# Dividing an attention's weights in the transpose, by a diagonal matrix from ScalarE

## The chip, the cores and the metric

The kernel runs on one core of one Trainium2 chip. The metric is the device time of one execution in microseconds (us), as the median of several runs. The core has five engines that run side by side and wait for each other by semaphores: TensorE (PE in the profile, and PEld for its weight loads), VectorE (DVE), ScalarE (ACT), GpSimd (POOL) and SyncE (SP), which issues most of the transfers (DMA).

## The reference

One layer of an encoder on 1024 tokens of width 1024, in float32: a normalised and modulated input is projected to queries, keys and values of two attentions that run in parallel, their outputs are projected, gated, merged and added to x, and a gated feed-forward network follows. The dilated attention has three groups of four heads, and its outputs are combined by their log-sums; the neighbourhood attention has eight heads on a grid of 16 rows of 64 columns, with a bias for each head. What the change touches is the softmax of the latter:

```python
scores = jnp.einsum('brqhd,brkhd->bhrqk', qg, kn).astype(f32) * (dh ** -0.5) + bias[None]
scores = jnp.where(mask, scores, NEG_INF)
p = jax.nn.softmax(scores, axis=-1).astype(v.dtype)
o = jnp.einsum('bhrqk,brkhd->brqhd', p, vn)
```

## The kernel before, in words

Large products are made in three passes: each operand is split into a rounded high part on ScalarE (`whi`, L118) and the remainder on VectorE or GpSimd (`wlo`, L119), and high x high, high x low and low x high are added up in PSUM. The products that touch the softmax weights P (L495, L510) take plain float32 operands.

The attentions are cut into ten units of two heads. Units 0 to 5 are the dilated groups (kinds 0, 1 and 2, two units each), units 6 to 9 the neighbourhood attention (kind 3, "the fourth kind"). A loop over n makes the steps: step n projects one tile of 128 tokens of unit n // 8 (`proj_chunk`, L305, 24 matmuls into a bank `ps_d`), and beside it runs the attention of items of earlier units. From step 80 on, gate products (L705) stand in the place of the projection, for twelve steps.

An item of the fourth kind is 128 queries of two heads against two key blocks (first and last item of a unit) or three (the six between): 22 key blocks a unit, 88 in four units, 176 for two heads. An item passes through three steps:

- In its first step, `at_scores` multiplies q and k on TensorE (L469, into `ps_s`). Then `at_qk`, once for each head: VectorE adds the bias and finds the maximum (L483), ScalarE takes exp and the sum (L484), VectorE takes the reciprocal of the sum (L486, into column 2 of `sx`) and divides P by it (L487).
- In its second step, `at_turn` transposes P block by block on TensorE against the identity `ident` (L495, into a bank `ps_t`), and PT is copied out of the bank by ScalarE for the first head (L501) and by VectorE for the second (L499).
- In its third step, `at_pv` multiplies PT with v (L510, into `ps_v`), ScalarE copies the result (L513) and issues its transfer (L514).

P is a tile of 512 columns in four buffers; the fourth kind uses at most 384 of them. Each name of a PSUM bank has two buffers. `ps_t` is shared: behind the turns of a step, the dilated groups' results are combined through it (`combine_step`: L665 on TensorE; L673, L675 and L676 on VectorE), and so are sums of the modulation (L271 on TensorE), whose running sum VectorE makes (L294) from rows `wa` that arrive by DMA. The same step turns the q and k of the tile projected before (L370, into `ps_v`), and splits them (L392 and L393 on ScalarE, L394 and L395 on VectorE). `proj_post` normalises the tile just projected (L323, L324 and L343 on ScalarE; L326, L328 and L130 to L134 mostly on VectorE).

On TensorE the order is as written in the code: half of the projection, scores, PV, turns of q and k, turns of P, the other half with L271 and L665 in or behind it. On the other engines a scheduler sets the order in this part of the program, from its own estimate of times; each engine then runs its list strictly in that order.

A product against a diagonal matrix is also made at the start of the kernel: four of eight tiles of x are scaled so (L232, with the diagonal `xd`), the other four are turned with the identity (L234).

Of the kernel before, what the change touches and what calls it, by code (L numbers as in the profile page):

```python
# [12 lines left out]
AF = mybir.ActivationFunctionType  # L13
ALU = mybir.AluOpType
# [29 lines left out]
def hybrid_layer(ctx: ExitStack, tc: tile.TileContext, x, colp, wada1, wada2, bada2, wqkv, wg, wpa, wpb,  # L44
                 wo, w1, w2, hgain, ropeg, rope, rbias, bmask, g2r, out):
    nc = tc.nc
# [28 lines left out]
    def bank(tag):  # L75
        return ps.tile([128, 512], F32, tag=tag, name="ps_" + tag)
# [9 lines left out]
    ident = const.tile([128, 128], F32, name="ident")  # L86
# [5 lines left out]
    for i in (0, 2):  # L92
        nc.vector.scalar_tensor_tensor(hg[:, i:i + 1], hg[:, i:i + 1], 0.125, hg[:, i + 1:i + 2],
                                       op0=ALU.mult, op1=ALU.mult)
# [213 lines left out]
    def urgent(off):  # L308
        def deco(f):
            def g(*a):  # L310
                with tc.high_priority(off):
                    return f(*a)
            return g
        return deco
# [157 lines left out]
    @urgent(AQ)  # L472
    def at_qk(I, h):
        U, nq = I.U, I.nq
        nk = I.nkb * 128
        pS = I.pS[h]
        P = I.P[h] = ap_.tile([128, 512], F32, tag="p", bufs=4, name="P")
        if U.kind < 3:
            nm, sm = U.st[:nq, I.item, h:h + 1], U.st[:nq, I.item, 2 + h:3 + h]
        else:  # L480
            sx = ap_.tile([128, 3], F32, tag="sx", bufs=4, name="sx")
            nm, sm = sx[:nq, 0:1], sx[:nq, 1:2]
        nc.vector.tensor_tensor_reduce(P[:nq, :nk], pS[:nq, :nk], I.masks[h], -1.0, 3.0e38, ALU.add, ALU.min, nm)  # L483
        nc.scalar.activation(P[:nq, :nk], P[:nq, :nk], AF.Exp, scale=-1.0, bias=nm, accum_out=sm)  # L484
        if U.kind == 3:
            nc.vector.reciprocal(sx[:nq, 2:3], sm)  # L486
            nc.vector.tensor_scalar(P[:nq, :nk], P[:nq, :nk], sx[:nq, 2:3], None, op0=ALU.mult)  # L487

    @urgent(AT)
    def at_turn(I, h):  # L490
        nq, nkb = I.nq, I.nkb
        P = I.P[h]
        pt = bank("t")
        for i in range(nkb):
            nc.tensor.transpose(pt[:, i * 128:i * 128 + nq], P[:nq, i * 128:(i + 1) * 128], ident[:nq, :nq])  # L495
        PT = I.PT[h] = ap_.tile([128, 4, 128], F32, tag="pT", bufs=4, name="PT")
        src = pt.rearrange("p (b q) -> p b q", q=128)[:, :nkb, :nq]
        if h:
            nc.vector.tensor_copy(PT[:, :nkb, :nq], src)  # L499
        else:  # L500
            nc.scalar.activation(PT[:, :nkb, :nq], src, AF.Copy)  # L501
# [413 lines left out]
    for n in range(6, 92):  # L915
# [55 lines left out]
        if n >= PAIRED or n % 2 or n < 10:  # L971
            for I in cur:
                if I.__class__ is Cluster:
                    cl_scores(I)
                    cl_qk(I)
                else:
                    at_scores(I)
                    at_qk(I, 0)
                    at_qk(I, 1)
            for I in done:  # L980
                (cl_pv if I.__class__ is Cluster else at_pv)(I)
            for j in range(0, len(turns), 2):
                qk_turns(turns[j:j + 2], "s" if n < 10 else "v")
            for I in prev:
                if I.__class__ is Cluster:
                    cl_turn(I)
                else:
                    at_turn(I, 0)
                    at_turn(I, 1)
# [263 lines left out]
    for t in range(8):  # L1253
        pbs = [bank("dsv"[t % 3]) for _ in range(2)]
        ko = KFIRST if t == 0 else (KLAST if t == 7 else range(KT))
        for n, k in enumerate(ko):
            for hf in range(2):
                for a, b in PASS:
                    nc.tensor.matmul(pbs[hf], h2T[a][:, k, t * 128:(t + 1) * 128], wow[hf, k][b],  # L1259
                                     start=(n == 0 and (a, b) == PASS[0]), stop=(n == KT - 1 and (a, b) == PASS[2]))  # L1260
# [398 lines left out]
```

## Time and profile before

| | |
|---|---|
| median of 3 runs | 1508.05 us (1505.69 to 1510.28) |
| the profiled execution | 1513.64 us |
| its span, first to last instruction | 1511.8 us |
| mean granted TensorE clock | 0.997 |
| attention of the fourth kind, first to last turn of P (L495) | 375.6 to 610.2 us |
| instructions of L487, VectorE's division of P | 64 |

The profile is of one execution. Times are from the span's start. A view of groups gives for each: line, engine, operation, output<-input, shapes and count, then busy time in us and the mean of one in ns, then the engine's idle time just before them and what ended it. A view of the timeline gives start and length in us, engine, line and count, with idle time in brackets. The duration of a matmul in the trace runs from its issue to its end, and the next one is issued long before that, so the distance from start to start is its pace.

### The profile page before, as it was taken

The page shows a single profiled execution, that of the slowest core. Times are in us where ns is not written, and L with a number is a line of the kernel's source. Part 1 is how long each engine was busy: PE and PEld are TensorE (multiplying, and loading weights), DVE is VectorE, ACT ScalarE, POOL GpSimd, SP SyncE. Part 2 cuts the span into 40 slices and gives each one's busy share as a digit, 9 for nine tenths or more (in the row PEclk, how much of TensorE's full clock was granted, in tenths as well). Part 3 has the DMA queues.
Part 4 walks back from the last instruction along what each step waited for, and adds up shares of the span by engine and source line. Part 5 has one row for each costly group of instructions (what it writes and reads, how often), then busy time and mean ns, then how long its engine had stood idle before and what let it go on. Part 6 is the DMA issues. An engine that isn't in the chain of part 4 may idle for free.

```text
span 1511.8 us, 24199 instructions
## 1 busy us (share of the span) xinstructions
PE 1486.6 (98%) x8156; PEld 1266.7 (84%) x8156; DVE 1087.9 (72%) x2265; ACT 669.9 (44%) x1691; POOL 535.6 (35%) x540
## 2 busy tenths in 40 slices
PE   8999999999999999999999999999999999999998
PEld 7999989998888877788888888888888888887886
DVE  6868777767888744466665497788767777599468
ACT  5656656555645554245532344233222333344442
POOL 0432333221100040001351311677767776104464
PEclk9999999999999999999999999999999999999999
DMA  9626444645235164833553235335433334798343
GB/s 365 232 80 190 144 145 145 190 137 166 76 114 176 47 192 135 308 106 123 176 178 143 87 96 182 119 132 180 157 130 105 109 108 146 269 366 288 99 150 103
DMA packets 150637, 241.65 MB, mean 160 GB/s; under 512 B 26464, under 2 KB 69088, under 8 KB 149744
## 3 DMA queue, kind: packets, MB, share of 16 engines
q1 hardware_dynamic: 131936, 226.45, 45.7%
q10 hardware_dynamic: 18576, 13.64, 2.8%
q8 instruction: 65, 1.06, 0.3%
q14 instruction: 60, 0.49, 0.1%
HBM read 179.89 MB, written 60.15 MB: 159 GB/s over the span
## 4 chain that ended last, share of the span: by engine, by line
PE 79%; DMA 8%; DVE 7%; ACT 3%; issue 2%; POOL 1%; SPq 0%; ACTq 0%; DVEq 0%
PE ps_d L305 11%; PE ps_v L1324 7%; PE ps_d L1324 7%; PE ps_s L1324 7%; PE ps_t L1324 6%; PE ps_d L705 4%; PE ps_s L1494 3%; PE ps_d L1494 3%; DMA wa<-in_wada_dram 3%; PE ps_v L1494 2%; PE ps_t L1494 2%; PE ps_s L1259 2%; PE ps_d L1259 2%; DVE wlo L119 2%; PE ps_v L1259 1%
## 5 line engine op out<-in xcount | busy, mean ns | idle before, releaser
L119 POOL TENSOR_TENSOR wlo<-raw,whi 128x512 fp32r<-128x512 f32 (+2 forms) x133 | 172.5, 1310 | 467.4 <-ACT whi L118 428.8
L118 ACT ACTIVATE whi<-raw 128x512 fp32r<-128x512 f32 (+1 forms) x348 | 203.9, 599 | 261.4 <-PE ps_s L1494 39.4
L305 PE MATMUL ps_d<-whi,hT 128*128 128x384 f32 x1152 | 312.0, 342 | 0.6 <-ACT vs L343 0.6
L119 DVE TENSOR_TENSOR wlo<-raw,whi 128x512 fp32r<-128x512 f32 (+1 forms) x215 | 181.9, 859 | 77.1 <-ACT whi L118 72.5
L305 PEld LDWEIGHTS ps_d<-whi,hT 128*128 128x128 f32 x1152 | 210.8, 189 | 6.1 <-ACT vs L343 4.4
L305 PE MATMUL ps_d<-wlo,hT 128*128 128x384 f32 x576 | 193.8, 337 | 2.4 <-DVE wlo L119 2.1
L305 PEld LDWEIGHTS ps_d<-wlo,hT 128*128 128x128 f32 x576 | 109.2, 190 | 3.1 <-DVE wlo L119 2.4
L118 ACT ACTIVATE whi<-ws 128x512 fp32r<-128x512 f32 x65 | 40.8, 628 | 128.2 <-DVE ws L1341 85.4
L1274 POOL TENSOR_TENSOR e<-e,c 128x512 f32<-128x512 f32 x44 | 68.8, 1563 | 61.0 <-DVE c L1404 36.8
L335 POOL TENSOR_TENSOR ra<-qn,rtab 128x64 f32<-128x64 f32 x48 | 16.2, 338 | 154.5 <-DVE qn L328 137.5
L119 POOL TENSOR_TENSOR wlo<-m,whi 128x512 fp32r<-128x512 f32 x35 | 51.3, 1477 | 54.2 <-ACT whi L118 54.2
L1272 ACT ACTIVATE e<-e 128x512 f32<-128x512 f32 x44 | 27.4, 630 | 85.2 <-DVE e L1407 58.1
L548 ACT ACTIVATE P<-P,st 128x256 f32<-128x256 f32 (+2 forms) x100 | 45.8, 459 | 36.9 <-DVE st L546 36.9
L705 PE MATMUL ps_d<-hT,whi 128*128 128x512 f32 x192 | 60.5, 397 | 0.0
L129 ACT ACTIVATE ry<-ss,eps 128x4 f32<-128x4 f32 (+1 forms) x88 | 26.3, 298 | 75.0 <-DVE ss L326 62.5
L1324 PE MATMUL ps_v<-h2T,whi 128*128 128x512 f32 x192 | 59.2, 389 | 0.0
L1324 PE MATMUL ps_s<-h2T,whi 128*128 128x512 f32 x192 | 59.1, 389 | 0.0
L294 DVE SCALAR_TENSOR_TENSOR acc<-wa,cact,acc 128x512 f32<-128x512 f32 x56 | 42.0, 750 | 21.0 <-DMA wa<-in_wada_dram 20.8
L484 ACT ACTIVATE P<-P,sx 128x384 f32<-128x384 f32 (+1 forms) x64 | 37.1, 581 | 44.9 <-DVE sx L483 44.7
L1324 PE MATMUL ps_d<-h2T,whi 128*128 128x512 f32 x184 | 56.7, 390 | 0.0
L119 DVE TENSOR_TENSOR wlo<-ws,whi 128x512 fp32r<-128x512 f32 x45 | 50.6, 1125 | 8.1 <-ACT whi L118 8.1
L1273 DVE TENSOR_TENSOR e<-e 128x512 f32<-128x512 f32 x44 | 42.5, 974 | 16.6 <-ACT e L1272 16.6
(445 smaller groups left out, 3956.9 us busy)
## 6 DMA issues: line engine op xcount, KB each, us to landing
raw<-in_w_dram SPq DMA_DIRECT2D x139, 256.0 KB
ga_d<-e SPq DMA_DIRECT2D x77, 256.0 KB
raw<-ga_d SPq DMA_DIRECT2D x77, 256.0 KB
wa<-in_wada_dram SPq DMA_DIRECT2D x32, 512.0 KB
raw<-in_wqkv_dram SPq DMA_DIRECT2D x80, 192.0 KB
m<-in_w_dram SPq DMA_DIRECT2D x44, 256.0 KB
raw<-in_wg_dram SPq DMA_DIRECT2D x42, 256.0 KB
xt<-in_x_dram SPq DMA_DIRECT2D x16, 512.0 KB
```

The source lines that it names most:

```text
L118: nc.scalar.activation(hi[:, :n], r, AF.Copy)
L119: (eng or nc.gpsimd).tensor_sub(lo[:, :n], r, fview(hi[:, :n]))
L294: nc.vector.scalar_tensor_tensor(ada_acc[c], wa, cact[:, kk:kk + 1], ada_acc[c], op0=ALU.mult, op1=ALU.add)
L305: nc.tensor.matmul(pd[:, :384], tok(a, k, t), U.w[k][b][:, :384], start=(k == 0 and i == 0), stop=(k == KT - 1 and i == 2))
L484: nc.scalar.activation(P[:nq, :nk], P[:nq, :nk], AF.Exp, scale=-1.0, bias=nm, accum_out=sm)
L548: nc.scalar.activation(C.P[h][:nq, c], C.P[h][:nq, c], AF.Exp, scale=-1.0, bias=nm, accum_out=sm)
L705: nc.tensor.matmul(st["p"], gw[i, br][j][a][:, kk * 128:(kk + 1) * 128], hT[b][:, k, hs], start=(k == 0 and q == 0), stop=(k == 7 and q == 2))
L1259: nc.tensor.matmul(pbs[hf], h2T[a][:, k, t * 128:(t + 1) * 128], wow[hf, k][b], start=(n == 0 and (a, b) == PASS[0]), stop=(n == KT - 1 an ...
L1273: nc.vector.tensor_mul(sg, sg, a)
L1274: nc.gpsimd.tensor_mul(sg, sg, up)
L1324: nc.tensor.matmul(pb, w[p][:, k * 128:(k + 1) * 128], b[q][:, k], start=(k == 0 and i == 0), stop=(k == 3 and i == 2))
L1494: nc.tensor.matmul(pb[m], o[0][a][:, m * 128:(m + 1) * 128], o[1][b], start=(k == 0 and i == 0), stop=(k == HT - 1 and i == 2))
```

## The change

For the fourth kind, VectorE no longer divides P. ScalarE instead writes a diagonal matrix into the unused columns 384 to 511 of the P tile: the identity with each row scaled by the reciprocal sum of that query. The transpose of P becomes an ordinary product of P with this diagonal, which transposes and divides in one. The other kinds keep the transpose against the identity. The rest of the program is as before; lines below the change are four higher (L499 becomes L503, L501 becomes L505, L513 becomes L517, L673 becomes L677).

```diff
         nc.scalar.activation(P[:nq, :nk], P[:nq, :nk], AF.Exp, scale=-1.0, bias=nm, accum_out=sm)
         if U.kind == 3:
             nc.vector.reciprocal(sx[:nq, 2:3], sm)
-            nc.vector.tensor_scalar(P[:nq, :nk], P[:nq, :nk], sx[:nq, 2:3], None, op0=ALU.mult)
+            nc.scalar.activation(P[:, 384:512], ident, AF.Identity, scale=sx[:, 2:3])
...
         pt = bank("t")
         for i in range(nkb):
-            nc.tensor.transpose(pt[:, i * 128:i * 128 + nq], P[:nq, i * 128:(i + 1) * 128], ident[:nq, :nq])
+            if I.U.kind == 3:
+                nc.tensor.matmul(pt[:, i * 128:(i + 1) * 128], P[:, i * 128:(i + 1) * 128], P[:, 384:512],
+                                 start=True, stop=True)
+            else:
+                nc.tensor.transpose(pt[:, i * 128:i * 128 + nq], P[:nq, i * 128:(i + 1) * 128], ident[:nq, :nq])
```

The scheduler orders VectorE and ScalarE anew around it. On VectorE, in the first step with a combine (near 420 us in the profile), the rows before are these; `P_6178` and `P_6184` are the two heads of the item in its first step, `PT_6217` is the second head's PT of the item in its second step:

```order
L134 SCALAR_TENSOR_TENSOR ry_6138<-rz_6139,ry_6138 128x4
L486 RECIPROCAL sx_6179<-sx_6179 128x1
L328 TENSOR_TENSOR qn_6131<-qn_6131,ry_6138 128x256
L487 TENSOR_SCALAR P_6178<-P_6178,sx_6179 128x256
L486 RECIPROCAL sx_6185<-sx_6185 128x1
L499 COPY PT_6217<-ps_t_6213 128x384
L487 TENSOR_SCALAR P_6184<-P_6184,sx_6185 128x256
L394 SCALAR_TENSOR_TENSOR qk_5316<-ps_v_6200,hg_87,qk_5316 128x2x64
L395 TENSOR_TENSOR qk_5316<-ps_v_6200,qk_5316 128x2x64
L673 TENSOR_TENSOR oacc_6050<-ut_6051,ps_t_6234 128x512
```

And of the change, at the same place on VectorE:

```order
L134 SCALAR_TENSOR_TENSOR ry_6138<-rz_6139,ry_6138 128x4
L328 TENSOR_TENSOR qn_6131<-qn_6131,ry_6138 128x256
L486 RECIPROCAL sx_6179<-sx_6179 128x1
L486 RECIPROCAL sx_6185<-sx_6185 128x1
L394 SCALAR_TENSOR_TENSOR qk_5316<-ps_v_6200,hg_87,qk_5316 128x2x64
L395 TENSOR_TENSOR qk_5316<-ps_v_6200,qk_5316 128x2x64
L503 COPY PT_6217<-ps_t_6213 128x384
L677 TENSOR_TENSOR oacc_6050<-ut_6051,ps_t_6234 128x512
```

The two divisions are gone, and PT's copy has moved behind the two instructions that split q and k. On ScalarE, in the same step, the rows before are these:

```order
L484 ACTIVATE P_6178,sx_6179<-P_6178,sx_6179 128x256
L513 ACTIVATE stg_6197<-ps_v_6190 128x128
L484 ACTIVATE P_6184,sx_6185<-P_6184,sx_6185 128x256
L392 ACTIVATE qk_5316<-ps_v_6200,hg_87 128x2x64
L393 ACTIVATE qk_5316<-ps_v_6200 128x2x64
L514 DMA o_d_75<-stg_6197 128x128
L501 ACTIVATE PT_6211<-ps_t_6207 128x384
L323 ACTIVATE sq_6241<-ps_d_6157 128x256
```

And of the change, at the same place on ScalarE:

```order
L484 ACTIVATE P_6178,sx_6179<-P_6178,sx_6179 128x256
L484 ACTIVATE P_6184,sx_6185<-P_6184,sx_6185 128x256
L517 ACTIVATE stg_6197<-ps_v_6190 128x128
L392 ACTIVATE qk_5316<-ps_v_6200,hg_87 128x2x64
L393 ACTIVATE qk_5316<-ps_v_6200 128x2x64
L487 ACTIVATE P_6178<-ident_89,sx_6179 128x128
L505 ACTIVATE PT_6211<-ps_t_6207 128x384
L487 ACTIVATE P_6184<-ident_89,sx_6185 128x128
L518 DMA o_d_75<-stg_6197 128x128
L323 ACTIVATE sq_6241<-ps_d_6157 128x256
```

The two diagonals stand on either side of the first head's copy of PT, and the output's transfer is issued behind them. TensorE's list differs only in the operands of L495: the second operand is P's own last 128 columns in place of `ident`.

## The prediction

> **What bounds the kernel now.** The page comes first: its busy shares, and the chain of work that ended last.
>
> ```profile
> PE 1486.6 (98%) x8156; PEld 1266.7 (84%) x8156; DVE 1087.9 (72%) x2265; ACT 669.9 (44%) x1691; POOL 535.6 (35%) x540
> PE 79%; DMA 8%; DVE 7%; ACT 3%; issue 2%; POOL 1%; SPq 0%; ACTq 0%; DVEq 0%
> ```
>
> TensorE is busy nearly always and holds 79% of the chain; VectorE holds 7%. These are means over many stages, so the second view is the table of stretches. The change touches only the attention of the fourth kind, between 374 and 616 us. Columns: length, then busy time (with instruction count) of PE, PEld, DVE, ACT and POOL, the granted clock, DMA share, GB/s.
>
> ```profile
> 400.00:440.00 40.00, 38.16 (x273) 34.10 (x273) 34.98 (x112) 21.51 (x75) 5.67 (x5) 0.96 0.48 148
> 440.00:480.00 40.00, 39.43 (x294) 34.41 (x291) 36.23 (x120) 21.79 (x76) 3.66 (x3) 1.00 0.42 125
> 480.00:520.00 40.00, 36.22 (x255) 32.04 (x255) 32.41 (x104) 19.84 (x71) 2.59 (x2) 0.96 0.34 103
> 520.00:560.00 40.00, 40.00 (x249) 31.66 (x248) 20.61 (x68) 21.38 (x62) 13.98 (x11) 1.00 0.51 152
> 616.00:1512.00 896.00, 888.22 (x3948) 733.67 (x3946) 647.78 (x854) 330.22 (x575) 402.86 (x277) 1.00 0.48 160
> ```
>
> Up to 520 us VectorE is nearly full too (36.23 of 40); after that it is half idle, while TensorE is full. Behind 616 us TensorE is busy 888 of 896 us: what the stage loses or gains reaches the end. A busy PE can hide gaps, since each matmul's recorded duration overlaps the next. So the third view is the timeline (start, length, engine, line, count): does TensorE issue at its own pace?
>
> ```profile
> 440.38 0.44 PE L370 MATMUL ps_v<-ident,qn 128*128 128x128 f32 x2
> 440.66 0.82 PE L495 MATMUL ps_t<-ident,P 128*128 128x128 f32 x6
> 441.23 0.42 PE L305 MATMUL ps_d<-whi,hT 128*128 128x384 f32 x1
> ```
>
> The six turns of one item follow the two turns of q and k without a gap, and the projection follows them. In an ordinary step the order of TensorE's own instructions sets the time. Its true stalls in the stage are in the view of waits (who waited for whom, total us, times, longest; 372 to 617 us):
>
> ```profile
> PE ps_t L665 <- DVE PT L499: 3.7, 2, 1.9
> PE ps_t L495 <- DVE oacc L676: 1.9, 1, 1.9
> PE ps_v L370 <- DVE qn L328: 1.0, 1, 1.0
> PE ps_t L271 <- DVE PT L499: 0.4, 1, 0.4
> PE ps_t L665 <- ACT PT L501: 0.2, 1, 0.2
> ```
>
> These are 7.2 us, nearly all on VectorE. Two stretches above have a clock of 0.96: 0.04 x 40 = 1.6 us of full speed lost in each, and the timeline shows it right behind a long stall (498.75) as slow matmuls:
>
> ```profile
> 496.03 0.51 PE L305 MATMUL ps_d<-whi,hT 128*128 128x384 f32 x2
> ...
> 498.75 0.66 PE L665 MATMUL ps_t<-ident,fb 128*128 128x128 f32 x4 [1.86 <-DVE PT L499]
> ...
> 501.05 0.84 PE L305 MATMUL ps_d<-whi,hT 128*128 128x384 f32 x2
> ```
>
> A pair that took 0.51 us takes 0.84. So the stage holds 7.2 + 2 x 1.6 = **10.4 us** that a lighter VectorE could at most give back.
>
> **The change part by part: TensorE.** Per key block and head, a turn against the identity (L495) becomes a real float32 product of P with the diagonal. The trace has that product already, with the same shapes: x against a diagonal, L232 (count, then ns min/median/max, first and last start).
>
> ```profile
> L232 PE MATMUL ps_d<-xd,xt x32: 275/275/377, 9.2 to 16.5; 128*128 128x128 f32 x32
> ...
> L232 PE MATMUL ps_v<-xd,xt x16: 275/275/275, 11.1 to 12.8; 128*128 128x128 f32 x16
> ...
> L232 PE MATMUL ps_s<-xd,xt x16: 275/275/377, 12.9 to 14.7; 128*128 128x128 f32 x16
> ```
>
> ```profile
> 11.12 1.95 PE L232 MATMUL ps_v<-xd,xt 128*128 128x128 f32 x16
> ```
>
> The program has 176 turns (4 head pairs x 22 key blocks x 2 heads) and the trace 110 + 66 = 176 (the table below). Of L232 it has 32 products (four token tiles of eight), and the trace 32 + 16 + 16 = 64: a float32 product runs as two instructions. Their pace: (1.95 - 0.275) / 15 = 0.112 us, so 0.224 a product; a turn's pace is (0.82 - 0.273) / 5 = 0.110. Each block costs 0.114 us more, and **176 x 0.114 = +20.1 us**, 0.68 us in a step of six. Nothing lies over it: TensorE is the engine that is waited for. By place:
>
> ```profile
> 374.00:520.00 146.00, 15.49 (x110) 12.62 (x110) 0.98 0.35 106
> 520.00:616.00 96.00, 9.67 (x66) 7.15 (x66) 1.00 0.51 153
> ```
>
> 110 blocks (12.5 us) fall where VectorE is nearly full, 66 (7.5 us) where it isn't.
>
> The Trainium skill, "TensorE: Matmul & The Clock Gate", section Back-to-back issue gap, gives about 81 ns a matmul for a sustained stream of loads and matmuls of 128 columns. By it the term would be, as an estimate, 176 x (0.162 - 0.110) = 9.2 us; the rows here show 112 ns for float32, and the row decides.
>
> **VectorE and ScalarE.** VectorE loses 64 divisions:
>
> ```profile
> L487 DVE TENSOR_SCALAR P<-P,sx 128x384 f32<-128x384 f32 x48 | 23.4, 488 | 1.2
> ...
> L487 DVE TENSOR_SCALAR P<-P,sx 128x256 f32<-128x256 f32 x16 | 7.7, 489 | 0.1
> ```
>
> 23.4 + 7.7 = 31.1 us of busy time, which counts only through the stalls above. ScalarE gains 64 activations of 128x128. The nearest rows are these:
>
> ```profile
> L392 ACT ACTIVATE qk<-ps_v,hg 128x128 fp32r<-128x128 f32 x23 | 10.9, 475 | 0.4 <-PE ps_v L370 0.3
> ...
> L513 ACT ACTIVATE stg<-ps_v 128x128 f32<-128x128 f32 x32 | 8.4, 261 | 8.8 <-PE ps_v L510 8.7
> ```
>
> So 64 x 0.26 = 16.7 us to 64 x 0.475 = 30.4 us; it cannot be below nothing, as nothing is taken from ScalarE. I take 17, by L513, the same types in plain order. It costs the end nothing while its cover holds: ScalarE is idle 18 of 40 us, and the turn that reads the diagonal comes a step later. Where the division of an item ended (421.15 + 0.34), that item's turn began only at 427.17:
>
> ```profile
> 421.15 0.34 DVE L487 TENSOR_SCALAR P<-P,sx 128x256 f32<-128x256 f32 x1
> ```
>
> ```profile
> 427.17 0.60 PE L495 MATMUL ps_t<-ident,P 128*128 128x128 f32 x4
> ```
>
> That leaves 5.7 us for ScalarE. The diagonal now waits for the reciprocal on VectorE, and behind it in ScalarE's queue stand PT's copy (L501) and the copies of the next projection (L323, L324, L343). If VectorE is late, PT's copy is late and with it the bank that L665 wants; up to all 17 us would then be on the path. I take 0.
>
> **How much of the 10.4 us comes back.** Four places, from the timeline of VectorE, and one of ScalarE:
>
> ```profile
> 373.96 0.61 DVE L487 TENSOR_SCALAR P<-P,sx 128x256 f32<-128x256 f32 x2
> 374.48 0.41 DVE L326 TENSOR_REDUCE ss<-sq 128x4 f32<-128x256 f32 x1
> ```
>
> ```profile
> 417.33 1.54 DVE L294 SCALAR_TENSOR_TENSOR acc<-wa,cact,acc 128x512 f32<-128x512 f32 x2 [1.35 <-DMA wa<-in_wada_dram]
> ...
> 420.36 0.35 DVE L487 TENSOR_SCALAR P<-P,sx 128x256 f32<-128x256 f32 x1
> 420.62 0.15 DVE L486 RECIPROCAL sx<-sx 128x1 f32<-128x1 f32 x1
> ```
>
> ```profile
> 465.35 0.43 DVE L394 SCALAR_TENSOR_TENSOR qk<-ps_v,hg,qk 128x128 fp32r<-128x128 f32 x1
> 465.68 0.40 DVE L395 TENSOR_TENSOR qk<-ps_v,qk 128x128 fp32r<-128x128 f32 x1
> 465.97 0.30 DVE L656 COPY fb<-fe 128x256 f32<-128x256 f32 x1
> ```
>
> ```profile
> 486.05 0.75 DVE L294 SCALAR_TENSOR_TENSOR acc<-wa,cact,acc 128x512 f32<-128x512 f32 x1 [0.76 <-DMA wa<-in_wada_dram]
> ```
>
> ```profile
> 496.18 0.63 ACT L118 ACTIVATE whi<-raw 128x512 fp32r<-128x512 f32 x1 [1.64 <-DMA raw<-in_wg_dram]
> ```
>
> At 375 the two divisions stand right ahead of what TensorE waits for: 374.48 - 373.96 = 0.5 of the 1.0 us comes back. At 421 only one division goes (0.26, start to start), and PT's copy is put behind L394 and L395, 0.62 us; the root there is a DMA 1.35 us late. At 487 no division is in the way, and a DMA is 0.76 late. At 499 ScalarE sat behind a DMA for 1.64. So most of the stalls are late transfers, which a lighter VectorE doesn't mend. Longer steps may: each gives a transfer 0.68 us more. I take half of 421 and 499 with their slow clock (3.7 + 3.2 = 6.9, so 3.4), 1.0 of 1.9 at 487, 0.5 at 375 and 0.3 of the rest: **-5.2 us**, between 0 and -10.4.
>
> **Sum.** +20.1 - 5.2 = +14.9. The profiled execution took 1513.64 us (span 1511.8 and 1.8 around it); 1528.5 on that scale. It lay 5.6 above the median of the runs shown, 1508.05, so the forecast is 1508.05 + 14.9 = **1523.0 us**.
>
> **Rivals.** *No stall goes, or new ones come.* The late transfers and the new place of PT's copy speak for it. +20.1 gives 1528.2; with two more stalls like that at 499 (1.9 + 1.6 each) +27.1, 1535.
>
> *All stalls go.* VectorE is 2 x 0.488 = 0.98 us lighter a step and steps are longer. +20.1 - 10.4 = +9.7: 1517.8. Against it: the roots are transfers.
>
> *VectorE sets the length of a step up to 520 us (the other side).* Then the 12.5 us of products there fall into time that TensorE has to wait anyway, 7.5 remain, and the stalls go: 7.5 - 10.4 = -2.9, 1505.2, no change. It decides if TensorE stands idle 0.68 us in every step of that stretch. For it: 36.23 of 40 us busy. Against it: 39.43 of 40 on TensorE and no gap around L495 at 440 us. The Trainium skill, "Perfetto Trace Analysis", section Optimizing Scalar/DVE Operations, says that moving work to Scalar may make sense where DVE is saturated; by that rule this rival holds, and the trace bears out the busy share, but not the waits.
>
> *The product costs no more than a turn* (one pass, so the change does less than it says): 176 x 0.002 - 5.2 = -4.8, 1503.2, faster. L232's doubled count is against it.
>
> **How the numbers follow.** Forecast 0.55, no stall goes or new ones 0.20, all go 0.15, VectorE sets the step 0.06, one pass 0.04. A measurement of this kernel can tell about 0.3%, 4.5 us, from no change: slower is the first three, 0.90; same 0.06; faster 0.04. The range runs from 1514, with room under "all go" for a cheaper product and the 2.3 us by which the runs before lie off their median, to 1533, most of the way through "new ones"; the last two rivals (0.10) and the top of the second are left out.
>
> **What would show it.** The product's line with 352 instructions at a pace of 0.112 us, and steps 0.7 us longer with no gap around it, show the main term; 176 instructions, or a pace near 0.055, refute it. VectorE some 31 us lighter in 374 to 616, ScalarE some 17 heavier. Waits of TensorE in the stage near 3.6 instead of 7.2 us, and at most one slow-clock stretch, show the share that comes back. Waits of PT's copy on ScalarE's diagonal, or stalls behind 616 us that shrink by more than 1 us, would make it wrong.

## The result, and the profile after

| | before | after |
|---|---|---|
| median | 1507.91 us (4 runs, 1505.69 to 1510.28) | 1525.45 us (4 runs, 1524.51 to 1529.0) |
| the profiled execution | 1513.64 us | 1526.08 us |
| its span | 1511.8 us | 1524.3 us |
| first to last turn or product of P | 375.6 to 610.2 us | 373.8 to 622.1 us |

The ratio is 1.0117, with an interval of 1.0101 to 1.0133. By the medians the change is 17.5 us slower. The forecast was 14.9 us slower, 1523.0 in a range of 1514 to 1533.

The page after, busy shares and the chain that ended last:

```profile
PE 1505.2 (99%) x8332; PEld 1285.6 (84%) x8332; DVE 1065.1 (70%) x2201; ACT 686.9 (45%) x1755; POOL 536.1 (35%) x540
PE 79%; DMA 8%; DVE 6%; ACT 3%; issue 2%; POOL 1%; SPq 1%; ACTq 0%; DVEq 0%
```

TensorE has 8332 - 8156 = 176 instructions more; VectorE has lost 64, ScalarE has gained 64. The same stretches after (columns as before the change: length, then busy us and count of PE, PEld, DVE, ACT, POOL, the clock, DMA share, GB/s):

```profile
400.00:440.00 40.00, 39.23 (x293) 35.69 (x292) 32.21 (x99) 24.30 (x84) 5.39 (x5) 1.00 0.46 145
440.00:480.00 40.00, 39.97 (x297) 35.09 (x296) 30.72 (x101) 23.97 (x82) 3.30 (x3) 1.00 0.36 107
480.00:520.00 40.00, 38.60 (x287) 34.63 (x287) 31.13 (x97) 22.21 (x77) 2.58 (x2) 1.00 0.40 121
616.00:1512.00 896.00, 893.03 (x3982) 737.62 (x3981) 643.77 (x853) 332.01 (x581) 403.03 (x277) 1.00 0.49 161
```

VectorE has fallen from 36.23 to 30.72 of 40 us in the middle one, ScalarE has risen from 21.79 to 23.97, and TensorE has only become fuller. The clock of 0.96 in two stretches is gone. An ordinary step on TensorE (timeline: start, length, engine, line, count) and the product's line (ns min/median/max, first and last start):

```profile
449.44 0.44 PE L370 MATMUL ps_v<-ident,qn 128*128 128x128 f32 x2
449.71 1.50 PE L496 MATMUL ps_t<-P 128*128 128x128 f32 x12
450.97 0.42 PE L305 MATMUL ps_d<-whi,hT 128*128 128x384 f32 x1
```

```profile
L496 PE MATMUL ps_t<-P x352: 275/275/377, 373.8 to 622.1; 128*128 128x128 f32 x176
```

Where six turns took 441.23 - 440.66 = 0.57 us up to the next line's start, twelve instructions for the same six blocks take 450.97 - 449.71 = 1.26, again without a gap: 0.69 us more in a step. And the waits of TensorE in the stage (who waited for whom, total us, times, longest):

```profile
PE ps_t L669 <- DVE PT L503: 1.2, 1, 1.2
PE ps_v L370 <- DVE qn L328: 1.2, 1, 1.2
PE ps_t L669 <- ACT PT L505: 0.8, 1, 0.8
PE ps_t L496 <- DVE rv L130: 0.2, 1, 0.2
```

That is 3.4 us in place of 7.2.

### The profile page after: what moved, and what is told of

It reads as the page before. It is cut to its first block, busy times and chain, and to the rows that moved or that the text cites. A ratio compares the mean times of both kernels' runs of the same rounds, so it can differ in the third digit from the quotient of the medians.

```text
span 1524.3 us, 24580 instructions
## 1 busy us (share of the span) xinstructions
PE 1505.2 (99%) x8332; PEld 1285.6 (84%) x8332; DVE 1065.1 (70%) x2201; ACT 686.9 (45%) x1755; POOL 536.1 (35%) x540
## 4 chain that ended last, share of the span: by engine, by line
PE 79%; DMA 8%; DVE 6%; ACT 3%; issue 2%; POOL 1%; SPq 1%; ACTq 0%; DVEq 0%
PE ps_d L305 12%; PE ps_v L1328 7%; PE ps_d L1328 7%; PE ps_s L1328 7%; PE ps_t L1328 6%; PE ps_d L709 4%; PE ps_t L496 2%; PE ps_s L1498 2%; PE ps_d L1498 2%; PE ps_s L1263 2%; PE ps_d L1263 2%; PE ps_t L1498 2%; PE ps_v L1498 2%; DMA wa<-in_wada_dram 2%; DVE wlo L119 2%
```

## The experiments

Two questions were put. Is the second instruction of the product the whole cost, or have the diagonal, its wait and the new order a part? And what of the price came back, and by what: the lighter VectorE, or the longer steps? Ratios are to the kernel before, run beside each experiment on the same chip; 0.001 is 1.5 us. The median of before was not the same beside all of them (1507.9 to 1509.7 us), so runs are compared by their ratios.

| run | what differs from before | ratio | interval |
|---|---|---|---|
| the change | product, diagonal on ScalarE, no division on VectorE | 1.0117 | 1.0101 to 1.0133 |
| e1 | product against the identity, VectorE divides | 1.0117 | 1.01 to 1.0135 |
| e2 | turns, no division at all | 0.9996 | 0.9983 to 1.0009 |
| e3 | turns, ScalarE divides | 0.9958 | 0.9942 to 0.9974 |
| e4 | nothing; one more execution of before | - | - |
| e6 | the change, first two units | 1.0045 | 1.0029 to 1.0061 |
| e7 | the change, last two units | 1.0054 | 1.0039 to 1.007 |
| e8 | turns of P ahead of those of q and k | 0.9984 | 0.9972 to 0.9995 |
| e9 | the change, product in one instruction | 0.9971 | 0.9955 to 0.9987 |
| e10 | e3 and e8 | 0.9962 | 0.9947 to 0.9977 |
| e11 | e9 and e8 | 0.999 | 0.9976 to 1.0004 |
| e12 | each turn made twice | 1.0108 | 1.0091 to 1.0125 |

### e1: the product alone

```diff
-            nc.tensor.transpose(pt[:, i * 128:i * 128 + nq], P[:nq, i * 128:(i + 1) * 128], ident[:nq, :nq])
+            if I.U.kind == 3:
+                nc.tensor.matmul(pt[:, i * 128:(i + 1) * 128], P[:, i * 128:(i + 1) * 128], ident, start=True, stop=True)
+            else:
+                nc.tensor.transpose(pt[:, i * 128:i * 128 + nq], P[:nq, i * 128:(i + 1) * 128], ident[:nq, :nq])
```

> The turn of the fourth kind becomes the float32 product, but against the identity, and VectorE keeps its division. Theory A (the product's second instruction is the cost, 176 x 0.114 = 20.1 us, and a lighter VectorE gives a little back): with VectorE as heavy as before, 1508 + 20 less at most 3 for the longer steps, so 1525 to 1528, as long as the change or up to 3 us longer. Theory B (VectorE sets the length of a step up to 520 us): the products there are hidden, at most 1508 + 7.5 = 1516. Theory C (the cost of the change lies in ScalarE's diagonal and the wait for it): near 1508 here.

Measured: 1528.25 us, ratio 1.0117, the same as the change (before was at 1509.69 beside it). Its waits of TensorE in the stage:

```profile
PE ps_v L370 <- DVE qn L328: 1.5, 1, 1.5
PE ps_t L668 <- DVE PT L502: 1.5, 1, 1.5
PE ps_t L668 <- ACT PT L504: 1.0, 1, 1.0
PE ps_t L496 <- DVE oacc L679: 0.2, 1, 0.2
```

These are 4.2 us where before has 7.2 (5.8 in a second profile, e4), with VectorE as heavy as before. So the product by itself costs all that the change costs, and the stalls shrink without a lighter VectorE. Theories B and C fall: they asked for at most 1516 and for 1508.

### e2: no division, and e3: ScalarE divides

```diff
-            nc.vector.tensor_scalar(P[:nq, :nk], P[:nq, :nk], sx[:nq, 2:3], None, op0=ALU.mult)
```

> P of the fourth kind is not divided at all: the turns stay, VectorE loses its 64 divisions and nothing takes their place. Theory A: only the stalls can shrink, by about 5 of the 10.4 us that the profiled execution held, so 1501 to 1506. Theory B (VectorE sets the step): 64 x 0.3 to 0.49 us less on VectorE would show nearly in full up to 520 us, so 1490 to 1496. If the stalls are late transfers alone: 1507 to 1509.

```diff
-            nc.vector.tensor_scalar(P[:nq, :nk], P[:nq, :nk], sx[:nq, 2:3], None, op0=ALU.mult)
+            nc.scalar.activation(P[:nq, :nk], P[:nq, :nk], AF.Identity, scale=sx[:nq, 2:3])
```

> ScalarE divides P in place of VectorE, with the turns as before: 64 activations of some 0.58 us, 37 us more on ScalarE. Theory A: ScalarE is half idle and the turns come a step later, so it hides; the time is that of the kernel without division, 1502 to 1507. Theory C (work added to ScalarE in this stage costs the end): above 1512.

Measured: e2 1509.12 us, ratio 0.9996: taking 31 us of instructions off VectorE (25 us of its busy time, 1087.9 to 1062.7), and putting them nowhere, gains nothing that can be measured. Theory A's 1501 to 1506 did not come; the time lies near the range of "late transfers alone". e3 measured 1503.59, ratio 0.9958: 6 us faster, with as light a VectorE and a heavier ScalarE. The two differ in where the division is, and so in the order that the scheduler made. Most of the waits of e2 and then of e3:

```profile
PE ps_t L664 <- DVE PT L498: 3.9, 2, 2.1
PE ps_t L494 <- DVE oacc L675: 1.1, 1, 1.1
```

```profile
PE ps_t L665 <- DVE PT L499: 1.1, 1, 1.1
PE ps_t L495 <- ACT qk L393: 0.9, 1, 0.9
```

There are two long waits for PT's copy in e2 and one in e3. The first is in both: 2.1 us near 420 us in e2 and 1.1 us in e3, behind rows `wa` for which VectorE sat idle 3.17 and 2.06 us. The second, 1.8 us, is in e2 alone. VectorE's timeline there, in e2 and then in e3:

```profile
493.81 0.42 DVE L394 SCALAR_TENSOR_TENSOR qk<-ps_v,hg,qk 128x128 fp32r<-128x128 f32 x1
494.14 0.37 DVE L395 TENSOR_TENSOR qk<-ps_v,qk 128x128 fp32r<-128x128 f32 x1
494.44 0.41 DVE L498 COPY PT<-ps_t 128x256 f32<-128x256 f32 x1
```

```profile
490.51 0.41 DVE L499 COPY PT<-ps_t 128x256 f32<-128x256 f32 x1
...
492.32 0.45 DVE L394 SCALAR_TENSOR_TENSOR qk<-ps_v,hg,qk 128x128 fp32r<-128x128 f32 x1
492.66 0.40 DVE L395 TENSOR_TENSOR qk<-ps_v,qk 128x128 fp32r<-128x128 f32 x1
```

In e2 the copy stands behind the split of q and k; in e3 it stands ahead. ScalarE, which had sat idle for transfers in both (1.8 us in e2, 1.4 in e3), ended its part of the split in e3 (L393) only at 491.91, so that a copy behind the split could not have begun before 492.5. At this step an earlier place of one row goes with 1.8 us less stall, where 31 us less on VectorE had gained nothing. All waits of the stage together are 6.2 us in e2 and 3.0 in e3, and their stages from first to last turn 230.4 and 227.3 us; the rest of the 6 us is not explained by these.

### e4: the kernel before, profiled again

> The kernel before, unchanged, for a second profile. If its stalls of 7.2 us on TensorE and the two stretches at a clock of 0.96 belong to every execution, they show again and the span is near 1512. If they vary, the waits are shorter, the clock 1.00, and the span near 1506, which would mean that the change had less to give back in the median than in the profiled execution.

Measured: 1506.82 us in one execution, span 1505.0. The stage is shorter than in the first profile, the clock is 1.00 throughout it, and the waits are 5.8 us:

```profile
PE ps_t L665 <- DVE PT L499: 3.5, 2, 2.1
PE ps_v L370 <- DVE qn L328: 1.0, 1, 1.0
PE ps_t L495 <- DVE oacc L676: 0.7, 1, 0.7
PE ps_t L271 <- DVE PT L499: 0.4, 1, 0.4
PE ps_t L665 <- ACT PT L501: 0.2, 1, 0.2
```

```profile
L495 PE MATMUL ps_t<-ident,P x176: 272/273/329, 373.7 to 603.9; 128*128 128x128 f32 x176
```

From first to last turn it takes 603.9 - 373.7 = 230.2 us, where the first profile had 234.6. The change's 622.1 - 373.8 = 248.3 is 18.1 more than this: about the 17.5 of the medians. So the two stretches at a clock of 0.96 and 1.4 us of the waits do not belong to every execution. But this one isn't the typical one either: it is 2.9 us below the median of the 17 runs of before beside it. Their mean clock goes from 0.996 (the slowest, 1514.56 us) to 1.000 (the fastest, 1504.72), and in the runs of the change it is 0.999 or 1.000.

### e6 and e7: half of the units each

Each is the change under a condition: `pair < 2` in e6 and `pair >= 2` in e7, at both places of its diff.

> The change for the first two of the four units alone (88 of 176 products, in the stretch in which VectorE is nearly full). Theory A (each product costs its second instruction wherever it stands): 88 x 0.114 = 10.0 us less the 1 to 3 us that late transfers gain from longer steps, so 1514 to 1518 against 1507.9 before. Theory B (what falls into the full stretch is hidden): 1505 to 1509.

> The change for the last two units alone (88 products, mostly where VectorE is half idle and TensorE has no stalls). Theory A: +10.0 us with nearly nothing given back, 1516 to 1519. Together with the first two units' it should make the whole change's 17.5 us. Theory B: 1518 here and nothing for the first two.

Measured: 1517.28 us, ratio 1.0045 (+6.8 us at 1507.9), and 1518.72 us, ratio 1.0054 (+8.1). Against the medians of before beside them (1508.64) it is 8.6 and 10.1 us; the two ways of counting differ by 2 us. Nothing is hidden where VectorE is nearly full: theory B falls again. The first half may give back a little more than the second, as expected, but the intervals (some 2.4 us to each side) don't tell the two apart, nor their sum (14.9, or 18.7 by the medians) from the whole's 17.5.

### e9: the product in one instruction

```diff
-        P = I.P[h] = ap_.tile([128, 512], F32, tag="p", bufs=4, name="P")
+        P = I.P[h] = ap_.tile([128, 512], F32 if U.kind < 3 else F32R, tag="p", bufs=4, name="P")
```

> The change with P and the diagonal as fp32r, so that the scores, P and the diagonal are rounded; everything else as in the change. If the cost is that a float32 product runs as two instructions, the trace shows 176 in place of 352 and the time falls by at least 176 x 0.112 = 19.7 us from the change's 1525.5, to 1504 to 1507, or lower if one instruction is faster than a turn. If the cost were in the diagonal, the wait or the order, it stays above 1515.

Measured: 1504.7 us, ratio 0.9971. The diagonal, its wait and the lighter VectorE are all there, and the cost is gone: 1.0117 - 0.9971 = 0.0146, 22 us, where 176 x 0.112 = 19.7 was expected; the two intervals of 0.0016 don't tell these apart. The product's line (the view writes f32 for a product of either kind):

```profile
L496 PE MATMUL ps_t<-P x176: 272/276/328, 375.8 to 604.4; 128*128 128x128 f32 x176
```

### e8, e10 and e11: the copy ahead of the split

In each step of the fourth kind (`n >= PAIRED`) the loop over `turns` (with `qk_turns`) is moved behind the loop over `prev` (with `at_turn`):

```diff
-            for j in range(0, len(turns), 2):
+            for j in range(0, 0 if n >= PAIRED else len(turns), 2):
                 qk_turns(turns[j:j + 2], "s" if n < 10 else "v")
             for I in prev:
...
                     at_turn(I, 0)
                     at_turn(I, 1)
+            for j in range(0, len(turns) if n >= PAIRED else 0, 2):
+                qk_turns(turns[j:j + 2], "s" if n < 10 else "v")
```

> The kernel before, with the turns of P written ahead of the turns of q and k in each step of the fourth kind, so that VectorE copies PT before it splits q and k in every step; the same work. If the stalls of L665 on PT's copy come from the copy standing behind a split that waits for ScalarE, the stall of 1.9 us near 494 to 499 us goes and the time falls by 2 to 5 us, to 1503 to 1506. If the stalls are set by the late transfers alone: 1507 to 1509. Slower if q and k, now turned later, hold up the scores.

Measured: 1507.94 us, ratio 0.9984, 2.4 us faster with an interval of 0.8 to 4.2; the medians alone differ by 0.7 (before was at 1508.64 beside it), and 1507.94 itself lies in the range of "late transfers alone". At the step near 494 us the wait is 0.2 us, where the second profile of before had 2.1; this is the timeline of e8 and then of before:

```profile
494.16 0.66 PE L665 MATMUL ps_t<-ident,fb 128*128 128x128 f32 x4 [0.22 <-ACT PT L501]
```

```profile
493.98 0.66 PE L665 MATMUL ps_t<-ident,fb 128*128 128x128 f32 x4 [2.12 <-DVE PT L499]
```

The place of the copy is only a part of that difference. VectorE up to the copy, in the second profile of before and then in e8:

```profile
489.59 1.25 DVE L132 TENSOR_TENSOR rz<-ry,rv 128x4 f32<-128x4 f32 x1
...
491.72 1.17 DVE L133 SCALAR_TENSOR_TENSOR rz<-rz,ry 128x4 f32<-128x4 f32 x1
492.81 0.43 DVE L394 SCALAR_TENSOR_TENSOR qk<-ps_v,hg,qk 128x128 fp32r<-128x128 f32 x1
...
493.51 0.41 DVE L499 COPY PT<-ps_t 128x256 f32<-128x256 f32 x1
```

```profile
491.71 0.15 DVE L132 TENSOR_TENSOR rz<-ry,rv 128x4 f32<-128x4 f32 x1
...
492.73 0.53 DVE L133 SCALAR_TENSOR_TENSOR rz<-rz,ry 128x4 f32<-128x4 f32 x1
493.19 0.41 DVE L499 COPY PT<-ps_t 128x256 f32<-128x256 f32 x1
```

The split ahead of the copy took 493.51 - 492.81 = 0.70 us. Before it the rows L132 and L133 together took 1.74 us more than in e8, and each ends within 0.03 us of a subtraction of GpSimd (the last section comes back to this). So in these two executions two small rows that ran long make more of the difference than the copy's place. In the first profile of before they did not run long (0.16 and 0.31 us); there the split waited for ScalarE, and the copy with it:

```profile
497.58 0.44 DVE L394 SCALAR_TENSOR_TENSOR qk<-ps_v,hg,qk 128x128 fp32r<-128x128 f32 x1 [1.62 <-ACT qk L393]
```

In e8's list of waits stands one of 2.6 us for the copy elsewhere (near 421 us, where VectorE sat idle 3.24 us for `wa`; in the second profile of before it was 0.92):

```profile
PE ps_t L665 <- DVE PT L499: 2.6, 1, 2.6
```

> ScalarE divides P (as in the run in which it does so alone, 0.9958 of the time before) and the turns of P are written ahead of the turns of q and k (alone 0.9984). If the first gained because the copy of PT came ahead of the split at the step near 494 us, the second adds little: 1501 to 1504. If the two remove different stalls, 1499 to 1502. Above 1506 if the gain of the first came from its own order, which the new writing undoes.

> The one-instruction product (fp32r, with scores, P and diagonal rounded; alone 0.9971) with the turns of P ahead of the turns of q and k. TensorE has the same work as before, VectorE 31 us less, ScalarE 25 us more. If what is left of the stalls in the one-instruction run (1.3 us on PT's copy, 0.6 on q and k) is order: 1501 to 1504. If it is late transfers: as without, 1504 to 1506.

Measured: e10 1503.17 us, ratio 0.9962, as e3 alone, so the new writing adds nothing to it in all: e3 had put the copy ahead at that step by itself. No wait for the copy is left in e10, but its list has three others, of 1.6, 1.2 and 0.9 us. e11 1507.54, ratio 0.999, is not better than e9 (its interval reaches e9's) and above both ranges; its waits are 1.9 and 1.6 us, where e9 had 2.5 in all. Why was not followed further.

### e12: each turn twice

```diff
-            nc.tensor.transpose(pt[:, i * 128:i * 128 + nq], P[:nq, i * 128:(i + 1) * 128], ident[:nq, :nq])
+            for _ in range(2 if I.U.kind == 3 else 1):
+                nc.tensor.transpose(pt[:, i * 128:i * 128 + nq], P[:nq, i * 128:(i + 1) * 128], ident[:nq, :nq])
```

> The kernel before with each turn of the fourth kind made twice into the same place: 176 more instructions at a turn's pace of 0.110 us, 19.4 us of TensorE, no product, no diagonal, VectorE divides as before. If the change costs what its second instruction costs, and the 2 to 3 us that come back of it are what longer steps give to late transfers and late copies, this comes to 1508 + 17 = 1524 to 1526 too, with waits on VectorE near 4 us in place of 7.2. If what comes back hangs on the lighter VectorE: 1527 to 1528.

Measured: 1525.41 us, ratio 1.0108, +16.3 us of a gross 19.4, with waits of 1.5 + 1.2 + 1.0 + 0.2 = 3.9 us:

```profile
PE ps_t L666 <- DVE PT L500: 1.5, 1, 1.5
PE ps_t L666 <- ACT PT L502: 1.2, 1, 1.2
PE ps_v L370 <- DVE qn L328: 1.0, 1, 1.0
PE ps_t L496 <- DVE oacc L677: 0.2, 1, 0.2
```

176 more instructions on TensorE, as turns or as halves of a product, do what the change does, and about as much of the price comes back as there, with VectorE dividing all the while.

## Why the prediction was right, and what in it was mis-sized

- **TensorE, +20.1 us**: right. 352 instructions in place of 176, at (1.50 - 0.275) / 11 = 0.111 us each; a step is 0.69 us longer, 0.68 was forecast. e1 and e12 give the cost without the rest of the change, e9 gives the rest without the cost.
- **What comes back, -5.2 us**: the sign was right and the size was not. It was a half of the 10.4 us seen in one execution. That execution was 5.6 us above the median, as the prediction itself noted; the second profile has a clock of 1.00 throughout the stage and waits of 5.8 us. After the change there are 3.4, so 2.4 come back, and 20.1 - 2.4 = 17.7, against 17.5 measured. That is again one execution each, and so close a match is partly luck: a thousandth of the mean clock, which differs between the runs, is 1.5 us. From the profiled execution before it is 1526.08 - 1513.64 = 12.4, so that 7.7 of the 20.1 came back there; the forecast of 14.9 lies in the middle, 2.5 and 2.6 us from the two. The step that failed is the carrying over of a term, worked out from the stalls of a single execution, to the median of the runs.
- **By what it comes back**: the prediction gave longer steps most of the part and the lighter VectorE some (0.5 us at 375 us, 0.26 at 421). e2 shows no gain from the lighter VectorE alone, and at 375 us the wait is 1.2 after and 1.0 before. Longer steps suffice, as e1 and e12 show. By place, in the first profile of before, the second and after: near 421 us 1.8, 1.4 and 0.8; near 487 us 1.9, 0.7 and none; near 499 us 1.9, 2.1 and 1.2.
- **The 31 us of VectorE and the 17 of ScalarE**: VectorE's busy time fell by 22.8 us (1087.9 to 1065.1), not by 31, since the 31.1 adds up durations that overlap the next row's. ScalarE's rose by just 17.0 (669.9 to 686.9), but that is luck: a diagonal takes 395 ns, not 261, so 64 x 0.395 = 25 us, and overlap makes it less. It is hidden, as e9 shows:

```profile
L487 ACT ACTIVATE P<-ident,sx 128x128 f32<-128x128 f32 x64 | 24.6, 395 | 4.1 <-DVE sx L486 4.0
```

- **The signs that it named**: TensorE waits 0.8 us for ScalarE's copy of PT near 423 us, and a diagonal stands right ahead of that copy; but e1, with no diagonal, has 1.0 us there. Behind the stage nothing is gained: from the last turn to the end of the span 901.6 and 901.1 us in the two profiles of before, 902.2 after.
- **The rivals**: VectorE as the bound up to 520 us fell with e1, e2 and e6; the cheap product fell with the trace itself. "No stall goes", 1528.2, was 2.7 us too high, about as far off as the forecast was too low, though stalls did go. "All go" was too cheap by 7.6 us.
- **The rule of the Trainium skill** on moving work to Scalar where DVE is saturated ("Perfetto Trace Analysis", Optimizing Scalar/DVE Operations) was bound to the third rival. e3 does gain by moving the division to ScalarE, 6 us, but e2 gains nothing by leaving it out. So it is not the load on VectorE that held this stage; near 494 us the traces of e2 and e3 point to order in its place.

e3 beats both kernels: 0.9958 of the time before, at no cost on TensorE. That the place of PT's copy is a part of its gain is seen against e2 at the step near 494 us (1.8 us); the rest of the 6 us was not taken apart.

## What to carry to other kernels

Folding a scale into a transpose turns one instruction of TensorE into a real product, and in float32 that was two instructions here: where TensorE sets the pace, count its instructions first, and leave the scale on an engine with room. Removing work from an engine that is only nearly full can gain nothing (e2) where the others wait for it because of late transfers, the order of its list, or rows that are held up. And a term that is read from the stalls of one profiled execution has to be checked against a second and scaled to the median, since part of them differs from one execution to the next.

## What the runs showed of the hardware

An instruction of 128 columns has nearly the same pace on TensorE in the three forms seen here: 0.110 us for a float32 turn, 0.112 for half of a float32 product and, in e9, (0.86 - 0.276) / 5 = 0.117 for an fp32r product:

```profile
446.38 0.86 PE L496 MATMUL ps_t<-P 128*128 128x128 f32 x6
```

A short VectorE instruction can be held up by GpSimd. After the change, near 498 us, VectorE's timeline and then GpSimd's:

```profile
498.16 1.04 DVE L132 TENSOR_TENSOR rz<-ry,rv 128x4 f32<-128x4 f32 x1
...
500.34 1.33 DVE L328 TENSOR_TENSOR qn<-qn,ry 128x256 f32<-128x256 f32 x1
```

```profile
497.88 1.30 POOL L119 TENSOR_TENSOR wlo<-raw,whi 128x512 fp32r<-128x512 f32 x1 [27.03 <-ACT whi L118]
500.11 1.28 POOL L119 TENSOR_TENSOR wlo<-raw,whi 128x512 fp32r<-128x512 f32 x1 [0.93 <-ACT whi L118]
```

L132 takes 0.16 us in the median; here it ends at 499.20, with GpSimd's subtraction (499.18). L328, usually 0.4, ends at 501.67 against 501.39. In the second profile of before the two long rows shown with e8 end at 490.84 and 492.89, and GpSimd's subtractions at 490.82 and 492.87. Which row is held changes with the time at which the transfer ahead of the subtraction lands. The Trainium skill ("Perfetto Trace Analysis", Optimizing Scalar/DVE Operations) says that GPSIMD and DVE share an SBUF read port, which agrees; no run here tests that cause by itself. After the change PT's copy stands ahead of the split in this step and right behind L328, and TensorE still waits 1.2 us for it: the two rows, 0.9 us longer each, are enough for that.

A stall of TensorE is not always followed by a slow clock. In the first profile of before, stalls of 1.84 and 1.86 us were followed by a granted clock of 0.50 (422 to 424 us) and 0.53 (500 to 502 us). A stall of 2.12 us in the second profile and one of 2.55 us in e8 were not: the clock stayed at 1.00. What decides it, no run here shows.
